# A hybrid two-layer trunk: one branch for steep decays of all heads, with its results in memory, instead of a branch in each head

## Chip, cores and metric

The kernel runs on one core of a Trainium2 chip. The metric is the device time of one execution in microseconds (us). Its engines are TensorE (PE, with its weight loads shown apart as PEld), VectorE (DVE), ScalarE (ACT), GpSimd (POOL) and SyncE (SP), which issues nearly all DMA transfers. The time before is 1061.45 us, the median of 3 runs (1060.91 to 1062.27).

## What is computed

Sixteen learned meta tokens are put ahead of 512 tokens of width 1024 (528 rows in all). Layer 1 is gated linear attention (GLA) with 4 heads, layer 2 differential softmax attention with 8 heads and a shared relative-position bias. Each has a pre-norm, an input projection, a SiLU gate and an output projection. All inputs are float32. What the change touches lies in the first layer:

```python
def gla_chunk(S, inp):
    q, k, v, lg = inp
    b = jnp.cumsum(lg, axis=2)                      # log decay, per key channel
    rel = b[:, :, :, None, :] - b[:, :, None, :, :]
    decay = jnp.exp(jnp.where(causal[:, :, None], rel, -jnp.inf))
    attn = jnp.einsum('bhid,bhjd,bhijd->bhij', q, k, decay)
    o = (jnp.einsum('bhij,bhjv->bhiv', attn, v)
         + jnp.einsum('bhid,bhdv->bhiv', q * jnp.exp(b), S))
    ...
```

and, in the second layer, in the bias `table[t5_bucket(max(dist, 0))]`, which the kernel makes as a matmul of the table with a constant 0/1 matrix (`c_hot`).

## The kernel before

Activations are kept transposed, channels on the 128 partitions and the 528 rows along the free axis. A product in float32 is made of three products of split operands (high x high, high x low, low x high): `split` (L238, L239) makes the high part on ACT and the low part on DVE, both for weights and for activations. The GLA projections of heads 1 to 3 are done as `Unit`s of seven half-size products (L355, 128 x 264 columns), so that sums of weight blocks are made on DVE as well (L295).

**Order.** PE's order is written out by hand. A `Weaver` object `W` holds a queue of generators that yield pieces of projection work. The code for the attention of a head calls `W.fill(us)`, which issues about that many us of projection matmuls, `W.finish(gen)`, which issues them up to the end of a generator, and `W.settle()`, which runs the work that was deferred (the turning of v into token order). The other engines get their order from a scheduler with priorities. Weights (`raw`) come in by SP one or two tiles ahead, when DVE has released the buffer.

**A head of GLA** (L1102 on): z of the head and q, k of the next are queued as filler; `gla_scores` makes the decayed keys kd (L986, L987) and the scores within blocks of 128 (L993, L1001), masked and split into `s.am` (16 meta rows) and `s.a`; `gla_ready` makes the scores across blocks from kd (L1018); `gla_blocks` makes the outputs. `gla_scores` uses exp(b) and exp(-b) as separate factors, which holds only while the decay within a block stays above a limit. So the kernel tests the least decay (`fl`, L871, L872), sums the flag over the partitions with a matmul (L875), puts it into `fi` (L877) and loads it into a register of each engine (L1101). In each of the four heads `tc.If(steep > 0)` (L1122, L1123 in the profile) stands between `gla_scores` and `gla_ready`; its body, `steep_scores`, makes the scores and kd again by eight levels of masks, and overwrites `s.am`, `s.a` and `s.kd`. It uses `hT`, the residual stream, as working space and saves it in `hT_dr`. With these inputs the flag is zero and the body never runs; each engine jumps past it.

**Second-layer setup** (`second_layer_setup`, in head 1): the 0/1 matrix comes in two halves of 33 x 328 (L893), then a matmul for each (L898), a copy and a store to `bdr`, and lam from four vectors (L902 on).

Of the kernel before, what the change touches and what calls it, by code (L numbers as in the profile page):

```python
# [11 lines left out]
F32 = mybir.dt.float32  # L12
# [7 lines left out]
P = 128  # L20
D = 1024
NM = 16
# [162 lines left out]
def trunk(ctx, tc, x, meta, g_norm, gla_w_in, gla_w_gate_up, gla_b_gate, gla_gnorm, gla_w_out,  # L185
# [35 lines left out]
    def ps_tile():  # L221
        return T(ps_pool, [P, 512], F32, "ps")
# [649 lines left out]
    dve.tensor_scalar(fl[:, 1:2], fl[:, 0:1], DECAY_LIMIT, None, op0=ALU.is_lt)  # L872
    W.fill(2.0)
    pf = ps_tile()
    pe.matmul(pf[0:1, 0:1], fl[:, 1:2], one1, start=True, stop=True)  # L875
    fi = T(hp, [1, 1], I32, "fi")
    dve.tensor_copy(fi, pf[0:1, 0:1])  # L877

    bdr = T(dp, [D_HEADS, TLEN], F32, "bdr")
    hT_dr = T(dp, [P, KT, L], F32, "hTd")
    lam = cp.tile([P, 1], F32, name="lam")
    dgs = cp.tile([P, 2], F32, name="dgs")

    def second_layer_setup():
        tab = T(cp, [NBUCK + 1, D_HEADS], F32, "tab")
        dve.memset(tab, NEG)
        sp.dma_start(tab[:NBUCK], rel_bias)
        n = TLEN // 2  # L890
        hots = [tmp(), tmp()]
        for i in range(2):
            sp.dma_start(hots[i][:NBUCK + 1, :n], c_hot[:, i * n:(i + 1) * n])  # L893
        W.fill(4.0)
        for i in range(2):
            hot, bsb = hots[i], tmp()
            ps = ps_tile()
            pe.matmul(ps[:D_HEADS, :n], tab, hot[:NBUCK + 1, :n], start=True, stop=True)  # L898
            dve.tensor_copy(bsb[:D_HEADS, :n], ps[:D_HEADS, :n])
            sp.dma_start(bdr[:, i * n:(i + 1) * n], bsb[:D_HEADS, :n])  # L900
        lamb, lt = tmp()[:, :4 * P].rearrange("p (a b) -> p a b", a=4), tmp()[:, :2 * P].rearrange("p (a b) -> p a b", a=2)
        sp.dma_start(lamb, d_lam.partition_broadcast(P))  # L902
        dve.tensor_tensor(lt, lamb[:, 0::2, :], lamb[:, 1::2, :], op=ALU.mult)
        lam2 = T(cp, [P, 2], F32, "lam2")
        dve.tensor_reduce(lam2, lt, axis=AX.X, op=ALU.add)
        act.activation(lam2, lam2, AF.Exp)
        dve.tensor_tensor(lam, lam2[:, 0:1], lam2[:, 1:2], op=ALU.subtract)
        dve.tensor_scalar(lam, lam, LAM_INIT, None, op0=ALU.add)
        dve.tensor_scalar(dgs, dg_sb, 0.5 * (1.0 - LAM_INIT), None, op0=ALU.mult)

    def steep_scores(hd, s):


        sp.dma_start(hT_dr, hT)
        flat = hT.rearrange("p k c -> p (k c)")
        qk = flat[:, :2 * L].rearrange("p (a b) -> p a b", a=2)
        raw = flat[:, 2 * L:2 * L + D].rearrange("p (k c) -> p k c", k=KT)
        acc = tmp()
        dve.memset(acc, 0.0)
        for i in range(2):  # L920
# [23 lines left out]
            act.activation(e[:, :400], e[:, :400], AF.Exp, scale=-1.0 / TAU)  # L944
            dve.tensor_tensor(s.kd[:, i, :], qk[:, 1, :400], e[:, :400], op=ALU.mult)
            for lv, half in enumerate(MASKS):
                mk = T(tp, [P, P], F32, "mk", bufs=1)
                sp.dma_start(mk, c_levels[lv])
                for t0, n, nb in ((0, NM, 1), (NM, NR, 4)):
# [24 lines left out]
                    dve.tensor_tensor(acc[:c, t0:t0 + n], acc[:c, t0:t0 + n], r[:c, :n], op=ALU.add)  # L974
        split(s.a[0], s.a[1], acc[:, NM:])
        pm = ps_tile()[:32, :NM]
        pe.matmul(pm, ident[:NM, :32], acc[:NM, :NM], start=True, stop=True)
        split3(s.am, pm, 64)
        sp.dma_start(hT, hT_dr)

    @urgent
    def gla_scores(hd, s):
        s.a = [T(gp, [P, NR], F32R, f"a{i}") for i in range(2)]
        s.kd = T(gp, [P, 2, 400], F32, "kd")
        for i in range(2):
            dve.tensor_scalar(s.kd[:, i, :NM], s.ks[:, i, :NM], eL[:, 2 * hd + i, 0:1], None, op0=ALU.mult)  # L986
            dve.tensor_tensor(s.kd[:, i, NM:].rearrange("p (b c) -> p b c", b=3),  # L987
                              s.ks[:, i, NM:400].rearrange("p (b c) -> p b c", b=3),
                              eL[:, 2 * hd + i, 1:4].unsqueeze(2).to_broadcast([P, 3, P]), op=ALU.mult)
        s.am = T(gp, [M3, NM], F32R, "am")  # L990
        pm = ps_tile()[:32, :NM]
# [3 lines left out]
        dve.tensor_tensor(r[:32, :NM], pm, short[:, :NM], op=ALU.mult)  # L995
        split3(s.am, r[:32, :NM], 64)
        ps = ps_tile()
        for b in range(4):
            cs = slice(NM + b * P, NM + (b + 1) * P)
            for i in range(2):  # L1000
                pe.matmul(ps[:, b * P:(b + 1) * P], s.ks[:, i, cs], s.qs[:, i, cs], start=i == 0, stop=i == 1)  # L1001
        r = tmp()[:, :NR]
        dve.tensor_tensor(r.rearrange("p (b c) -> p b c", b=4), ps.rearrange("p (b c) -> p b c", b=4),
                          tri.unsqueeze(1).to_broadcast([P, 4, P]), op=ALU.mult)
        split(s.a[0], s.a[1], r)

# [92 lines left out]
    token_sums(5)  # L1099
    W.settle()  # L1100
    steep = nc.values_load(fi[0:1, 0:1], min_val=0, max_val=P)  # L1101
    for hd in range(G_HEADS):  # L1102
        s = heads[hd]
# [12 lines left out]
        if hd == 0:  # L1116
            W.fill(3.0)
        gla_scores(hd, s)
        W.fill(4.0)
        if W.queue:  # L1120
            W.finish(W.queue[0])
        W.settle()  # L1122
        with tc.If(steep > 0):  # L1123
            steep_scores(hd, s)
        W.fill(2.0)
        gla_ready(hd, s)
        W.finish()
        W.settle()
# [410 lines left out]
```

## Time and profile before

| | us |
|---|---|
| median of 3 runs | 1061.45 |
| the profiled execution | 1060.68 |
| its span, first to last instruction | 1058.9 |
| PE busy | 1019.0 |
| DVE busy | 719.7 |
| ACT busy | 545.2 |

Mean granted clock of TensorE: 0.991 of full. A page of the profile gives busy times by engine; the timeline gives single instructions with the time that the engine stood idle before them and, behind an arrow, what ended that time. "PEq" and "DVEq" are the sequencers of PE and DVE, which read instructions, do branches and register loads, and hand the rest on. "L1123" rows are those of the branch: COMPARE_BRANCH is the jump, EVENT_SEMAPHORE what an engine does where both ways meet. In windows, PE busy is given with its count, the granted clock, the share of the DMA engines' time and GB/s.

### The profile page before, as it was taken

What the parts mean: (1) busy time and instruction counts of PE and PEld (TensorE: products, weight loads), DVE (VectorE), ACT (ScalarE), POOL (GpSimd) and SP (SyncE); (2) the same over time, 40 slices, a digit from 0 to 9 for tenths busy, and PEclk for the clock granted to TensorE, in tenths of its full rate; (3) what the DMA queues carried; (4) which work ended last, traced back from release to release, by engine and by line L of the source; (5) the groups of instructions that cost most, each with busy time, mean ns of one, the idle gap of its engine ahead of it and who ended that gap; (6) DMA issues with size and microseconds to landing.
All of it is one profiled execution on the core that took longest, in us unless ns stands there. A gap on an engine that the chain in (4) does not pass through costs nothing.

```text
span 1058.9 us, 18333 instructions
## 1 busy us (share of the span) xinstructions
PE 1019.0 (96%) x7345; PEld 954.2 (90%) x7345; DVE 719.7 (68%) x1441; ACT 545.2 (51%) x1198; POOL 38.4 (4%) x68
## 2 busy tenths in 40 slices
PE   8898988999899998999999999999999999999997
PEld 7898887999889997999999898998989989989895
DVE  7877884678776886656447675754757648576685
ACT  6774753446544655536525454443544445454453
POOL 1000000000000000000000000000000000000001
PEclk8999998999999999999999999999999999999999
DMA  7222221233212322212431222222222221222212
GB/s 195 64 56 69 80 82 55 79 81 81 82 41 80 92 68 82 81 48 77 130 105 45 89 81 90 80 90 81 80 88 61 89 93 54 88 80 81 72 48 80
DMA packets 98995, 84.69 MB, mean 80 GB/s; under 512 B 5528, under 2 KB 87802, under 8 KB 98892
## 3 DMA queue, kind: packets, MB, share of 16 engines
q1 hardware_dynamic: 98892, 83.31, 26.2%
q8 instruction: 65, 1.06, 0.4%
q14 instruction: 38, 0.31, 0.1%
HBM read 81.18 MB, written 2.12 MB: 79 GB/s over the span
## 4 chain that ended last, share of the span: by engine, by line
PE 57%; DVE 3%; ACT 1%; POOL 0%; issue 0%; POOLq 0%; DVEq 0%
PE pp L346 32%; PE pp L325 7%; PE ps L325 6%; PE bx L799 2%; PE bv L799 1%; PE bx L355 1%; PE by L799 1%; PE ps L1337 1%; PE ps L710 1%; PE bv L355 1%; PE ps L1360 1%; PE by L346 1%; PE ps L1018 1%; PE bv L346 1%; PE by L355 1%; DVE wl L239 0%
## 5 line engine op out<-in xcount | busy, mean ns | idle before, releaser
L346 PE MATMUL pp<-x,wh 128*128 128x264 f32 (+1 forms) x1504 | 321.7, 323 | 0.0
L346 PEld LDWEIGHTS pp<-x,wh 128*128 128x128 f32 x1504 | 227.0, 188 | 15.5
L238 ACT ACTIVATE wh<-raw 128x512 fp32r<-128x512 f32 (+1 forms) x212 | 138.2, 681 | 122.4 <-PE pp L346 52.6
L346 PE MATMUL pp<-x,wl 128*128 128x264 f32 (+1 forms) x752 | 198.2, 319 | 0.0
L239 DVE TENSOR_TENSOR wl<-raw,wh 128x512 fp32r<-128x512 f32 (+1 forms) x212 | 156.2, 757 | 56.6 <-ACT wh L238 41.2
L346 PEld LDWEIGHTS pp<-x,wl 128*128 128x128 f32 x752 | 124.3, 188 | 10.5
L457 POOL TENSOR_TENSOR st<-st,mhalf 128x1 f32<-128x1 f32 (+1 forms) x52 | 31.6, 607 | 942.8 <-DVE st L456 942.8
L1325 ACT ACTIVATE p<-p,st 128x528 f32<-128x528 f32 (+3 forms) x64 | 36.4, 569 | 49.3 <-DVE st L1324 48.9
L325 PE MATMUL pp<-wh,x 128*128 128x256 f32 x320 | 61.3, 282 | 0.0
L355 PE MATMUL bv<-x,wh 128*128 128x264 f32 x320 | 47.7, 287 | 4.9 <-DVE ks L400 2.5
L325 PEld LDWEIGHTS pp<-wh,x 128*128 128x128 f32 x320 | 51.0, 189 | 0.1
L355 PE MATMUL bx<-x,wh 128*128 128x264 f32 x320 | 48.3, 289 | 2.4 <-ACT u L374 1.2
L355 PEld LDWEIGHTS bv<-x,wh 128*128 128x128 f32 x320 | 42.3, 188 | 6.1 <-DVE ks L400 3.1
L355 PEld LDWEIGHTS bx<-x,wh 128*128 128x128 f32 x320 | 42.7, 190 | 3.2 <-issue 1.6
L325 PE MATMUL pp<-wl,x 128*128 128x256 f32 x160 | 45.1, 282 | 0.0
L1322 DVE SCALAR_TENSOR_TENSOR p<-ps,qr,T 128x264 f32<-128x264 f32 (+3 forms) x80 | 36.5, 490 | 6.4 <-PE ps L325 6.4
L374 ACT ACTIVATE u<-bx 128x264 f32<-128x264 f32 x60 | 23.0, 383 | 29.6 <-PE bx L355 28.6
L239 DVE TENSOR_TENSOR aT<-ps,aT 128x512 fp32r<-128x512 f32 (+3 forms) x32 | 15.7, 489 | 31.8 <-ACT aT L238 31.6
L325 PE MATMUL ps<-k,q 128*128 128x264 f32 (+3 forms) x240 | 36.8, 294 | 0.0
L325 PEld LDWEIGHTS ps<-k,q 128*128 128x128 f32 x240 | 33.6, 188 | 0.8
L325 PE MATMUL ps<-v,aT 128*128 128x256 f32 x240 | 33.9, 282 | 0.0
L325 PEld LDWEIGHTS ps<-v,aT 128*128 128x128 f32 x240 | 32.1, 188 | 1.8
(399 smaller groups left out, 2205.6 us busy)
## 6 DMA issues: line engine op xcount, KB each, us to landing
raw<-in_diff_w_in_dram SPq DMA_DIRECT2D x32, 1024.0 KB, 5.8
raw<-in_gla_w_in_dram SPq DMA_DIRECT2D x48, 512.0 KB, 5.3
raw<-in_gla_w_out_dram SPq DMA_DIRECT2D x8, 1024.0 KB, 5.1
raw<-in_diff_w_out_dram SPq DMA_DIRECT2D x8, 1024.0 KB, 5.0
T<-bdr SPq DMA_DIRECT2D x8, 264.0 KB, 3.6
out_dram<-z SPq DMA_DIRECT2D x8, 256.0 KB, 2.0
v<-in_x_dram SPq DMA_DIRECT2D x2, 512.0 KB, 6.7
qs<-in_x_dram SPq DMA_DIRECT2D x1, 512.0 KB, 3.8
```

The costliest lines, as they stand in the source:

```text
L238: act.activation(hi, src, AF.Copy)
L239: dve.tensor_tensor(lo, src, hi.bitcast(F32), op=ALU.subtract)
L325: pe.matmul(ps, l, r, start=first and n == 0, stop=last and n == 2, **kw)
L346: pe.matmul(bank, a[:, k, :], b[k][:, n0 + i * nn:n0 + (i + 1) * nn], start=k == 0 and n == 0, stop=k == nk - 1 and n == 2)
L355: pe.matmul(bank[:, :HT], w[p][:, k * P:(k + 1) * P], x[q][:, k, :], start=first and i == 0, stop=i == len(PASSES) - 1, skip_group_check=n ...
L374: act.activation(t, self.bx[:, :HT], AF.Copy, scale=self.sc)
L457: pool.tensor_tensor(dst, dst, mhalf[:np_, :dst.shape[1]], op=ALU.pow)
L710: pe.transpose(pt[:, b * P:(b + 1) * P], vt[:, t0:t0 + n], ident)
L799: pe.matmul(banks[i][:, :HT], h.t[p][:, k, mm * P:(mm + 1) * P], s.y[q][k][:, i * HT:(i + 1) * HT], start=n == 0, stop=n == len(PASSES) - 1)
L1018: pe.matmul(o, s.kd[:, i, kc], s.qs[:, i, t0:t0 + n], start=i == 0, stop=i == 1)
L1322: dve.scalar_tensor_tensor(p[:, c0:c1], ps[:, :c1 - c0], qr[:, b:b + 1], s.T[:, c0:c1], op0=ALU.mult, op1=ALU.add)
L1325: act.activation(p[:, :nk], p[:, :nk], AF.Exp, bias=st[:, m:m + 1], accum_out=st[:, 2 + m:3 + m])
```

## The change

1. The flag's matmul and its copy move from behind the decays to behind the projections of q and k of head 0, with `W.fill(1.0)` ahead and `W.fill(3.0)` behind, next to the register load.
2. One `tc.If(steep > 0)` stands there, ahead of the loop over heads. Its body saves `hT`, runs `steep_scores` for all four heads, and restores `hT`. `steep_scores` now writes scores and kd of a head to memory (`steep_dr`) in place of `s.a`, `s.am` and `s.kd`.
3. In `gla_scores` of each head, two DMAs are issued by SP with a condition on the flag's register: one into `s.kd` behind its making, one into the masked scores `r` ahead of their splits. The scores of the meta rows and of the blocks now lie in one tile `r`.
4. In the loop, `W.fill(4.0)`, the `W.finish` of the first generator, `W.settle()`, the branch and `W.fill(2.0)` become one `W.fill(5.0)`.
5. The 0/1 matrix is loaded whole, one head sooner, by one DMA into the buffer of kd, behind `gla_ready` of head 0.

```diff
@@ -870,16 +870,13 @@
-    W.fill(2.0)
-    pf = ps_tile()
-    pe.matmul(pf[0:1, 0:1], fl[:, 1:2], one1, start=True, stop=True)
     fi = T(hp, [1, 1], I32, "fi")
-    dve.tensor_copy(fi, pf[0:1, 0:1])
...
+    steep_dr = [[T(dp, shape, F32, f"steep{hd}_{i}") for i, shape in enumerate(([P, L], [P, 2, 400]))] for hd in range(G_HEADS)]
@@ -888,14 +885,11 @@
-        hots = [tmp(), tmp()]
-        for i in range(2):
-            sp.dma_start(hots[i][:NBUCK + 1, :n], c_hot[:, i * n:(i + 1) * n])
         W.fill(4.0)
         for i in range(2):
-            hot, bsb = hots[i], tmp()
+            bsb = tmp()
             ps = ps_tile()
-            pe.matmul(ps[:D_HEADS, :n], tab, hot[:NBUCK + 1, :n], start=True, stop=True)
+            pe.matmul(ps[:D_HEADS, :n], tab, hot[:NBUCK + 1, i * n:(i + 1) * n], start=True, stop=True)
@@ -972,11 +966,8 @@
-        split(s.a[0], s.a[1], acc[:, NM:])
-        pm = ps_tile()[:32, :NM]
-        pe.matmul(pm, ident[:NM, :32], acc[:NM, :NM], start=True, stop=True)
-        split3(s.am, pm, 64)
-        sp.dma_start(hT, hT_dr)
+        sp.dma_start(steep_dr[hd][0], acc)
+        sp.dma_start(steep_dr[hd][1], kd)
@@ -987,22 +978,23 @@
+        sp.dma_start(s.kd, steep_dr[hd][1], cond=steep > 0, cond_hint=False)
...
-        split3(s.am, r[:32, :NM], 64)
...
-        r = tmp()[:, :NR]
-        dve.tensor_tensor(r.rearrange("p (b c) -> p b c", b=4), ps.rearrange("p (b c) -> p b c", b=4),
+        dve.tensor_tensor(r[:, NM:].rearrange("p (b c) -> p b c", b=4), ps.rearrange("p (b c) -> p b c", b=4),
                           tri.unsqueeze(1).to_broadcast([P, 4, P]), op=ALU.mult)
-        split(s.a[0], s.a[1], r)
+        sp.dma_start(r, steep_dr[hd][0], cond=steep > 0, cond_hint=False)
+        split3(s.am, r[:32, :NM], 64)
+        split(s.a[0], s.a[1], r[:, NM:])
@@ -1098,7 +1090,18 @@
     W.finish(first[-1])
     token_sums(5)
     W.settle()
+    W.fill(1.0)
+    pf = ps_tile()
+    pe.matmul(pf[0:1, 0:1], fl[:, 1:2], one1, start=True, stop=True)
+    dve.tensor_copy(fi, pf[0:1, 0:1])
+    W.fill(3.0)
     steep = nc.values_load(fi[0:1, 0:1], min_val=0, max_val=P)
+    with tc.If(steep > 0):
+        sp.dma_start(hT_dr, hT)
+        for hd in range(G_HEADS):
+            steep_scores(hd)
+        sp.dma_start(hT, hT_dr)
@@ -1114,16 +1117,13 @@
         if hd == 0:
-            W.fill(3.0)
+            W.fill(2.0)
         gla_scores(hd, s)
-        W.fill(4.0)
-        if W.queue:
-            W.finish(W.queue[0])
-        W.settle()
-        with tc.If(steep > 0):
-            steep_scores(hd, s)
-        W.fill(2.0)
+        W.fill(5.0)
         gla_ready(hd, s)
+        if hd == 0:
+            hot = T(gp, [P, TLEN], F32, "kd")
+            sp.dma_start(hot[:NBUCK + 1], c_hot)
```

What this does to the order on the engines is shown at three places. The first is PE in head 0, at the jump. Before, the branch stood in the middle of a product of the next unit (bx, weights wh), behind the scores; the row behind COMPARE_AND_BRANCH here is the first one behind the body:

```order
L355 MATMUL bx_1203<-x_9_85,wh_1180 128x264 [waits Activation_49]
L355 MATMUL bx_1203<-x_10_86,wh_1180 128x264
L355 MATMUL bx_1203<-x_9_85,wh_1180 128x264
L1123 COMPARE_AND_BRANCH
...
L355 MATMUL bx_1203<-x_10_86,wh_1180 128x264
```

In the changed kernel the scores come behind the branch, and the register load stands right ahead of it:

```order
L355 MATMUL bv_1132<-x_7_83,wl_1057 128x264
L1098 TENSOR_LOAD fi_964 [waits DVE_49]
L1099 COMPARE_AND_BRANCH
...
L355 MATMUL bv_1132<-x_7_83,wl_1057 128x264 x3
L355 MATMUL bx_1073<-x_165_1077,wh_1065 128x264 [waits Activation_49]
...
L985 MATMUL ps_3957<-qs_821,ks_995 32x16 [waits DVE_49,PE_49]
```

The jump is 54 matmuls of 264 columns and the score matmuls earlier in PE's order than before, next to the load of the flag, and the first use of a PSUM tile behind it (ps) waits for DVE.

The second place is SP in head 1, where the table of the setup and the transfers of the head are issued. Before (t are the halves of the 0/1 matrix and the vectors of lam, raw a weight tile):

```order
L247 DMA raw_2575<-in_gla_w_out_dram 128x4x512 [waits DMAHW4_49,DMAHW7_49,DMAHW3_49,DVE_49]
L893 DMA t_2544<-in_hot_dram 33x328 [waits DMAHW0_49,PE_49]
L893 DMA t_2545<-in_hot_dram 33x328 [waits PE_49]
L902 DMA t_2617<-in_diff_lam_dram 128x512 [waits DMAHW0_49,PE_49]
L900 DMA bdr_1000<-t_2607 8x328 [waits DVE_49]
```

and in the changed kernel (the ISA rows make the condition; t_4707 is r):

```order
L247 DMA raw_4643<-in_gla_w_out_dram 128x4x512 [waits DMAHW1_49,DMAHW4_49,DMAHW0_49,DVE_49]
L981 ISA
L981 DMA kd_4697<-steep_1_146_970 128x800 [waits DMAHW7_49,DVE_49,PE_49]
L894 DMA bdr_965<-t_4675 8x328 [waits DVE_49]
L894 DMA bdr_965<-t_4680 8x328 [waits DVE_49]
L896 DMA t_4685<-in_diff_lam_dram 128x512
L995 ISA
L995 DMA t_4707<-steep_0_145_969 128x528 [waits DMAHW6_49,DVE_49]
L247 DMA raw_4787<-in_gla_w_out_dram 128x4x512 [waits DMAHW3_49,DMAHW2_49,DVE_49]
```

The loads of the table are gone from here, and two conditional transfers stand among the weight loads. The third place is ACT in head 1, behind the scores. Before, the splits into am and a waited for DVE alone:

```order
L332 ACTIVATE am_2634<-t_2638 32x16 [waits DVE_49]
L333 ACTIVATE am_2634<-t_2638 32x16
L238 ACTIVATE a_464_2627<-t_2652 128x512 [waits DVE_49]
```

In the changed kernel they wait for the DMA queue, and stand behind the split of the next weights (wh):

```order
L238 ACTIVATE wh_4779<-raw_4402 128x1024 [waits PE_49,Activation_49]
L332 ACTIVATE am_4703<-t_4707 32x16 [waits DMAHW1_49]
L333 ACTIVATE am_4703<-t_4707 32x16
L238 ACTIVATE a_906_4695<-t_4707 128x512
L238 ACTIVATE v_890_4646<-ps_4793 128x4x128 [waits PE_49]
L332 ACTIVATE cm_4805<-ps_4808 32x128 [waits PE_49]
```

What moved: am and a were made ahead of the branch and ahead of wh; now they come behind wh, behind a transfer, and ahead of v and cm.

More of the change, by code (lines that the diff above doesn't have):

```diff
@@ L909, in second_layer_setup, with steep_scores @@
         dve.tensor_scalar(dgs, dg_sb, 0.5 * (1.0 - LAM_INIT), None, op0=ALU.mult)
-    def steep_scores(hd, s):
-        sp.dma_start(hT_dr, hT)
+    def steep_scores(hd):
         flat = hT.rearrange("p k c -> p (k c)")
@@ L917, in steep_scores @@
         raw = flat[:, 2 * L:2 * L + D].rearrange("p (k c) -> p k c", k=KT)
-        acc = tmp()
+        kd = flat[:, 2 * L + D:2 * L + D + 800].rearrange("p (a b) -> p a b", a=2)
+        acc = flat[:, 3 * L + D + 400:4 * L + D + 400]
         dve.memset(acc, 0.0)
@@ L944, in steep_scores @@
             act.activation(e[:, :400], e[:, :400], AF.Exp, scale=-1.0 / TAU)
-            dve.tensor_tensor(s.kd[:, i, :], qk[:, 1, :400], e[:, :400], op=ALU.mult)
+            dve.tensor_tensor(kd[:, i, :], qk[:, 1, :400], e[:, :400], op=ALU.mult)
             for lv, half in enumerate(MASKS):
```

## The prediction

> **What bounds the kernel now.** I read the page first, then the chain of work, then the timeline of TensorE alone (PE) up to 500 us, and last the rows of the branch.
>
> ```profile
> span 1058.9 us, 18333 instructions
> PE 1019.0 (96%) x7345; PEld 954.2 (90%) x7345; DVE 719.7 (68%) x1441; ACT 545.2 (51%) x1198; POOL 38.4 (4%) x68
> ```
>
> PE is busy 1019.0 of 1058.9 us, and the chain that ended last runs almost wholly through PE matmuls, so time is won only where PE stands still or runs slowly. The timeline of PE prints, in brackets, how long it stood before a row and for whom. These are its stops in the stretch that the change touches:
>
> ```profile
> 80.75 0.19 PE L875 MATMUL ps<-ones,fl 128*1 128x1 f32 x2 [1.51 <-DVE fl L872]
> 86.89 1.40 PE L355 MATMUL bx<-x,a11h 128*128 128x264 f32 x8 [0.63 <-DVE ks L698]
> 102.74 0.85 PE L355 MATMUL bx<-x,wh 128*128 128x264 f32 x5 [1.18 <-PEq L1123]
> 107.33 1.25 PE L355 MATMUL bx<-x,wh 128*128 128x264 f32 x8 [1.23 <-ACT u L374]
> ...
> 159.49 1.26 PE L898 MATMUL ps<-t,tab 33*8 33x328 f32 x2 [2.87 <-DMA t<-in_hot_dram]
> 175.74 0.85 PE L355 MATMUL bv<-x,wh 128*128 128x264 f32 x5 [1.20 <-PEq L1123]
> 180.72 0.60 PE L1018 MATMUL ps<-qs,kd 128*32 128x128 f32 x4 [2.19 <-DVEq L1123]
> ...
> 287.95 0.84 PE L355 MATMUL bv<-x,wh 128*128 128x264 f32 x5 [1.22 <-PEq L1123]
> 292.36 0.60 PE L1018 MATMUL ps<-qs,kd 128*32 128x128 f32 x4 [1.62 <-DVEq L1123]
> ...
> 400.85 0.84 PE L355 MATMUL by<-x,a12h 128*128 128x264 f32 x5 [1.67 <-PEq L1123]
> 405.38 0.60 PE L1018 MATMUL ps<-qs,kd 128*32 128x128 f32 x4 [1.73 <-DVEq L1123]
> ```
>
> L1123 is the branch, taken past its body once for each of four heads. PE stops twice each time: while its own queue jumps (PEq), and then, in heads 1 to 3, until VectorE (DVE) has passed the branch too. Head 1 also waits 2.87 us for the table of L893. That stop has a second price, which the windows of PE show (length, PE busy, granted clock, DMA share, GB/s):
>
> ```profile
> 33.22:36.63 3.41, 1.45 (x9) 1.00 0.00 0
> 36.63:40.05 3.42, 3.42 (x18) 0.50 0.03 5
> ...
> 156.10:159.51 3.41, 0.54 (x6) 1.00 0.83 317
> 159.51:162.93 3.42, 3.42 (x12) 0.50 0.22 66
> 162.93:166.34 3.41, 3.41 (x18) 0.50 0.09 22
> ...
> 398.45:401.86 3.41, 1.74 (x15) 1.00 0.67 190
> 401.86:405.27 3.41, 1.79 (x15) 1.00 0.50 127
> ```
>
> After a window with 0.54 us of work, and after one with 1.45, the clock was 0.50 for one or two windows; after 1.74 it stayed at 1.00. In this trace the line lies between 1.45 and 1.74 busy out of 3.41.
>
> **What goes in heads 1 to 3.** The three branches go: 1.20 + 2.19 + 1.22 + 1.62 + 1.67 + 1.73 = **9.63 us** of PE idle time. The table is fetched some 40 us before its use, and L893's successor needs no transfer there: **2.87 us**. With that the emptied window is gone, and so are two windows at half clock, full of PE work: half of 6.83 is **3.4 us**. One group shows that this is real, the same 16 matmuls in head 0 and in head 1:
>
> ```profile
> 91.48 2.05 PE L1001 MATMUL ps<-qs,ks 128*128 128x128 f32 x16
> 162.09 3.78 PE L1001 MATMUL ps<-qs,ks 128*128 128x128 f32 x16
> ```
>
> This group alone gives 3.78 - 2.05 = 1.73 us, which is the low bound of the term. Sum of the three: 15.9 us. What is late next there is nothing large: the stops of 0.4 to 0.9 us at the changes between product units, which the branch does not cause, stay.
>
> **What happens in head 0.** The flag's matmul (L875) is put later, behind 12 more matmuls; fl is long done by then, and the stop of 1.51 goes. But the next stop, 0.63 for ks, comes from DVE, which was busy without a gap there, so PE only arrives sooner and waits longer: I take 1.3 in place of 0.63, so 0.65 is given back. Then comes the single branch, and it has to be priced anew, because it stands elsewhere.
>
> ```profile
> L1123 PEldq COMPARE_BRANCH  x4: 3292/3324/3756, 99.2 to 396.9; - x4
> L1101 PEldq TENSOR_LOAD <-fi x1: 491/491/491, 86.9 to 86.9; - x1
> ...
> L1123 ACTq COMPARE_BRANCH  x1: 50/50/50, 101.3 to 101.3; - x1
> L1123 ACTq EVENT_SEMAPHORE  x1: 17/17/17, 101.8 to 101.8; - x1
> L1123 DVEq COMPARE_BRANCH  x1: 67/67/67, 101.9 to 101.9; - x1
> L1123 DVEq EVENT_SEMAPHORE  x1: 21/21/21, 104.9 to 104.9; - x1
> ...
> L1123 DVEq COMPARE_BRANCH  x1: 63/63/63, 175.5 to 175.5; - x1
> L1123 DVEq EVENT_SEMAPHORE  x1: 21/21/21, 180.6 to 180.6; - x1
> ...
> q14 instruction: 38, 0.31, 0.1%
> ...
> 101.49:104.90 3.41, 2.23 (x19) 1.00 0.03 10
> ...
> 176.58:179.99 3.41, 1.95 (x17) 1.00 0.44 168
> ...
> 88.94 1.00 SPq L254 DMA_DIRECT2D raw<-in_gla_w_in_dram  x2
> ...
> 91.25:94.66 3.41, 3.41 (x32) 1.00 0.89 246
> ```
>
> PE's queue is some 2.2 us ahead of its engine (it reaches the branch at 99.2; its engine, full until then, restarts at 102.74 after 1.18 idle), so of 3.3 us 1.2 remain. Now the load of the flag stands right at the branch: with its 0.49 and about 0.1 between the two, PE idles 3.3 + 0.6 - 2.2 = 1.7 to 1.8. And the place is worse. DVE's jump took 3.0 us in head 0 (101.9 to 104.9) with DMA at 0.03, but 5.1 in head 1 (175.5 to 180.6) with a weight load under way at 0.44: instructions come over the DMA engines too (the queue of that kind), so what the jump has to fetch seems to queue with the data. The new branch comes, by my count of the rows ahead of it, at about 90 us, some 2 us after a pair of weight loads is issued (at 88.94 before, about 87.5 with the two kd operations now behind the split that releases the buffer); those loads fill the DMA for about 4 us. PE's own four jumps all began before the loads of their time. I add 0.9, near the middle between nothing and DVE's 2.1: **2.7 us** idle at the branch (bounds 1.2, as now, and 3.9).
>
> 2.7 us without work can leave a window under 1.45 us busy: 3.41 - 2.7 = 0.7 if the stop falls into one window, up to 2.0 if the border halves it. I take one window at half clock, **1.7 us** (bounds 0 and 3.4). The Trainium skill (TensorE: Matmul & The Clock Gate, section "What's actually happening") lets the clock fall only after at least one idle window of about 3.4 us. By that rule the new branch would cost no clock and the sum would be 1.7 us lower; the window from 33.22, with 1.45 us of work in it, speaks against the rule.
>
> Behind the branch PE's first use of a PSUM tile waits until DVE has passed; I take 0.5 for that. And ACT is late with u, as it was at 107.33 (1.23): the table load of L767 and the new wait stand ahead of it; I take 0.7. Head 0 in all: 1.51 + 1.18 + 1.23 = 3.9 saved; 0.65 + 2.7 + 1.7 + 0.5 + 0.7 = 6.25 paid.
>
> **The eight conditional transfers.** No run shows a transfer that is skipped. Nearest rows:
>
> ```profile
> t<-in_diff_lam_dram SPq DMA_DIRECT2D x1, 256.0 KB, 3.6
> raw<-in_diff_w_in_dram SPq DMA_DIRECT2D x32, 1024.0 KB, 5.8
> a<-in_gla_w_in_dram SPq DMA_DIRECT2D x1, 64.0 KB, 7.3
> ...
> 425.84 1.46 PE by L355 x12
> 94.30 0.64 ACT L238 ACTIVATE a<-t 128x512 fp32r<-128x512 f32 x1
> ```
>
> So a skip costs between nothing and 3.6 us from issue to release; I take 2, somewhat nearer to the transfer of a similar tile. The transfer of kd is issued right after kd is written, some 10 us ahead of its first reader on PE: hidden. That of the scores (r, a tile t) is issued about 1.2 us after the last score matmul, and three kinds of work stand behind it: ACT's am and a, then ACT's v, cm and u, then PE's product that reuses bx. In heads 1 to 3 PE has 69 matmuls of 264 columns before that product, 69 x 1.46 / 12 = 8.4 us, and two groups of transposes and the first kd products, about 2 us: 10.4. ACT needs, as I estimate, 3.3 us from the landing on (five 32-row copies, a at 0.64, v and u of like size). So a landing up to 7.1, a skip of 5.9 us, is free. I book 0.2 for each of the four heads, 0.8, for queueing; if the cover were gone, each skip would cost its 2 us. On SP's queue the weight loads behind these transfers wait for buffers that DVE releases later than it writes r, so nothing of theirs is delayed. The table's load, now one DMA of both halves into the kd buffer, stands behind head 0's last kd product; kd of head 1 then waits for PE to have read the table, which happens before DVE's turn.
>
> **Sum.** 15.9 + 3.9 - 6.25 - 0.8 = 12.8 us. The profiled execution took 1060.68 (span 1058.9 and 1.8 around it), so 1047.9; the median of the runs shown is 0.77 higher: **1048.7**. The stages behind 500 us are bound by PE and move as a whole.
>
> **Rivals.** (1) The clock holds at the new branch, since the border of the windows, free of the program, may halve the stop or the fetch may not queue: 1.7 less, **1047.0**. (2) The clock still falls in head 1: the matmuls of the table use 33 rows and 8 columns, and after the window from 159.51, full by its record, the clock stayed at 0.50; such work may not count. Then 3.4 comes back: **1052**. (3) The jump is far, now that one body holds four heads: ACT, which passed one head's body in 0.5 us (101.3 to 101.8), stops 3 to 5 us as DVE does now, is late with am, a, wh and u, and PE waits some 2 to 3 us more: **1051**. The Trainium skill (Runtime: NRT & Kernel Launch, section "Instruction fetch mechanics") says that a taken branch whose target lies outside the two pages held forces a fetch before anything goes on; ACT's 0.5 us fits a target that was held, and no run here shows ACT with a farther one. (4) Slower: the skip is no skip in time. Each r then blocks ACT's queue in its order, with PE's product behind it; free up to 5.9 us, beyond that 1 us for 1 us in four heads. It eats the 12.8 from 5.9 + 3.2 = 9.1 us on; at 10 us, **1065**. The longest landing above is 7.3, which speaks against it. (5) The branches' cost was not the branches': DVE is busy too (68% over the span), and PE arrives sooner at splits that are not ready; half of 9.6 returns: **1053.5**.
>
> **How the numbers follow.** Forecast 0.35, rival 1 0.26, rival 2 0.10, rival 3 0.13, rival 5 0.08, rival 4 0.05, and 0.03 that nothing moves. All good bounds together give 1061.45 - 15.9 - 3.9 + 1.2, about 1042.5; rivals 2, 3 and 5 and the high bounds reach to 1055. The range is 1043 to 1054.5. 0.2%, or 2.1 us, is about what a measurement of this kernel can tell from no change; faster than that 0.92, within it 0.03, slower 0.05.
>
> **What would show it.** PE's stops with L1123's successor as releaser: one group near 91 us, of 1.7 to 3.9 us, and none in heads 1 to 3. The windows of PE: clock 1.00 from 100 us on; 0.50 in the window behind the new branch or not decides between forecast and rival 1. ACT's idle time before am in heads 1 to 3 below 2 us, and the first kd product without a DMA as releaser. A stop of PE for u or bx of over 1 us in each head, or total PE idle time before 500 us down by less than 6 us, would make the prediction wrong.

## The result and the profile after

The changed kernel takes **1049.75 us** (median of 4 runs, 1044.26 to 1052.15); the kernel before took 1061.18 beside it (4 runs, 1059.28 to 1062.27). The ratio is 0.9892, with a 95% interval of 0.9870 to 0.9915: 11.4 us less. The prediction was 1048.7, in a range of 1043 to 1054.5. The profiled execution took 1049.57 us, 1060.68 before.

The page's first lines of the kernel after:

```profile
span 1047.8 us, 18311 instructions
PE 1017.8 (97%) x7345; PEld 954.0 (91%) x7345; DVE 718.8 (69%) x1441; ACT 544.5 (52%) x1198; POOL 37.9 (4%) x68
```

The same 7345 matmuls, 1.2 us less busy time, and a span that is 11.1 us shorter: what went is mostly time in which PE stood. The view by windows, cut at the same places in both kernels (the matmul that waits for DVE's ks in head 0, then the first stop at L799, the products of the output weights, behind the scores of heads 1, 2 and 3), shows where. Columns: window, its length, PE busy (instructions), granted clock, DMA share, GB/s. First before, then after:

```profile
0.00:86.89 86.89, 77.40 (x568) 0.94 0.40 104
86.89:189.53 102.64, 92.41 (x678) 0.97 0.23 67
189.53:301.15 111.62, 106.62 (x832) 1.00 0.27 77
301.15:438.14 136.99, 130.96 (x1025) 1.00 0.28 78
438.14:1058.90 620.76, 611.59 (x4245) 1.00 0.25 80
```

```profile
0.00:84.64 84.64, 75.30 (x566) 0.96 0.41 107
84.64:186.57 101.93, 95.60 (x695) 0.95 0.24 67
186.57:296.07 109.50, 106.79 (x831) 1.00 0.28 78
296.07:427.22 131.15, 128.60 (x1010) 1.00 0.29 81
427.22:1047.80 620.58, 611.49 (x4245) 1.00 0.25 80
```

From top to bottom: 2.25, 0.71, 2.12, 5.84 and 0.18 us less. The last row, over half of the span, did not move. The second and the fourth have to be read together: 16 kd matmuls, 2.4 us of work, came over from the fourth row into the second (x64 there before, x80 now, while the fourth went from x56 to x40). Without that shift heads 0 and 1 gained 3.1, head 2 gained 2.1 and head 3 gained 3.4. Heads 2 and 3 gained about what their branches had cost (2.84 and 3.40); heads 0 and 1 gained much less than the table and head 1's branch (9.7) would give. PE's timeline after shows why (its stops of over 1 us between 80 and 450 us):

```profile
84.64 1.24 PE L355 MATMUL bx<-x,a11h 128*128 128x264 f32 x8 [1.64 <-DVE ks L698]
94.35 1.00 PE L355 MATMUL bv<-x,wl 128*128 128x264 f32 x3 [3.65 <-PEq L1099]
167.12 1.34 PE L355 MATMUL bv<-x,wh 128*128 128x264 f32 x8 [1.80 <-DVE t L398]
```

No stop has the branch as releaser in heads 1 to 3, and none waits for the table. The three that remain are the earlier wait for ks, the single branch (L1099), and one that nobody had foreseen, in head 1 at 167.12. The windows of PE around the last two:

```profile
86.18:89.59 3.41, 3.41 (x30) 1.00 0.67 186
89.59:93.00 3.41, 1.11 (x10) 1.00 0.57 134
93.00:96.41 3.41, 2.06 (x9) 0.50 0.07 16
96.41:99.83 3.42, 3.42 (x19) 0.50 0.00 0
164.69:168.10 3.41, 1.61 (x14) 1.00 0.01 2
168.10:171.51 3.41, 3.41 (x18) 0.50 0.00 0
```

Both stops lowered the clock: two windows at 0.50 behind the branch, one in head 1. At half clock work takes about twice as long (the 16 score matmuls of the prediction: 3.78 us against 2.05), so a window costs about half of its PE time: 1.0 us for the first of the three, which holds 2.06 us of work, and 1.7 for each of the others.

The new stop's cause stands in DVE's and SP's timelines after:

```profile
160.06 0.55 DVE L978 TENSOR_TENSOR kd<-ks,eL 128x384 f32<-128x384 f32 x1
...
165.31 0.43 DVE L897 TENSOR_TENSOR t<-t 128x256 f32<-128x256 f32 x1 [3.89 <-DMA t<-in_diff_lam_dram]
...
166.66 0.41 DVE L398 SCALAR_TENSOR_TENSOR t<-bv,u 128x264 f32<-128x264 f32 x1
```

```profile
155.43 0.37 SPq L247 DMA_DIRECT2D raw<-in_gla_w_out_dram  x1
160.74 0.09 SPq L981 DMA_DIRECT2D kd<-steep  x1
161.04 0.69 SPq L894 DMA_DIRECT2D bdr<-t  x2
161.78 0.36 SPq L896 DMA_DIRECT2D t<-in_diff_lam_dram  x1
```

SP issues in order. The conditional transfer into kd (L981) may go only when DVE has written kd, at 160.06 + 0.55; behind it in the queue stand two stores of the table (L894), which wait for DVE's copies of it (until 161.42), and then the load of the four lambda vectors (L896), which needs nothing and goes out 5 us later than it could. This load was late in the kernel before, too: it went out at 160.78, and DVE stood 2.09 us for it, but PE, held up by the table, did not wait for that. Now DVE multiplies these vectors (L897) and stands 3.89 us for them first; behind that, in DVE's order, is L398, a step of a product whose result PE waits for.

### The profile page after: what moved, and what is told of

It reads as the page before. It is cut to its first block, busy times and chain, and to the rows that moved or that the text cites. A ratio compares the mean times of both kernels' runs of the same rounds, so it can differ in the third digit from the quotient of the medians.

```text
span 1047.8 us, 18311 instructions
## 1 busy us (share of the span) xinstructions
PE 1017.8 (97%) x7345; PEld 954.0 (91%) x7345; DVE 718.8 (69%) x1441; ACT 544.5 (52%) x1198; POOL 37.9 (4%) x68
## 3 DMA queue, kind: packets, MB, share of 16 engines
q1 hardware_dynamic: 98848, 83.31, 26.7%
HBM read 83.90 MB, written 2.12 MB: 82 GB/s over the span
## 4 chain that ended last, share of the span: by engine, by line
PE 77%; DVE 7%; ACT 2%; issue 2%; DMA 2%; POOL 1%; SPq 0%; POOLq 0%; DVEq 0%; ACTq 0%
PE pp L346 32%; PE ps L325 8%; PE pp L325 7%; PE bx L355 6%; PE bx L799 4%; PE bv L355 4%; PE by L355 3%; PE bv L799 2%; PE by L799 2%; PE ps L1010 2%; PE ps L710 1%; DMA raw<-in_gla_w_in_dram 1%; DVE wl L239 1%; PE ps L1337 1%; POOL st L457 1%
## 5 line engine op out<-in xcount | busy, mean ns | idle before, releaser
L239 DVE TENSOR_TENSOR wl<-sum,wh 128x1024 fp32r<-128x1024 f32 x20 | 24.4, 1221 | 14.5 <-ACT wh L238 9.6
```

The lines of the kernel that those rows point to most:

```text
L239: dve.tensor_tensor(lo, src, hi.bitcast(F32), op=ALU.subtract)
```

## The experiments

Each kernel was timed beside the kernel before. The last three columns are from the profiled execution alone: "branch" is PE's longest stop at the single branch in us, "windows" counts the half-clock windows between 80 and 450 us (1.7 us each where PE works through them), and "idle" is all the time in us that PE stands from the wait for ks in head 0 to the first L799 of head 3. The kernel before has two such windows and 21.3 us of idle time there, the kernel after three and 11.6.

| run | median us (range) | before beside it | ratio (95% interval) | branch | windows | idle |
|---|---|---|---|---|---|---|
| table only | 1055.28 (1053.69 to 1059.33) | 1059.46 | 0.9963 (0.9949 to 0.9977) | - | 1 | 18.6 |
| branch only | 1053.75 (1050.25 to 1055.13) | 1059.46 | 0.9940 (0.9920 to 0.9960) | 4.18 | 4 | 14.5 |
| no conditional transfers | 1047.07 (1045.53 to 1049.46) | 1059.46 | 0.9886 (0.9867 to 0.9905) | 3.95 | 1 | 10.7 |
| lambda sooner | 1047.11 (1043.94 to 1047.80) | 1059.46 | 0.9870 (0.9849 to 0.9890) | 4.21 | 1 | 12.1 |
| after again | 1048.86 (1046.79 to 1052.16) | 1059.95 | 0.9904 (0.9887 to 0.9922) | 3.48 | 1 | 11.3 |
| branch later | 1046.05 (1045.92 to 1046.86) | 1059.95 | 0.9868 (0.9852 to 0.9885) | 1.15 | 1 | 10.7 |
| empty body | 1040.53 (1039.52 to 1040.81) | 1059.95 | 0.9814 (0.9799 to 0.9828) | none | 0 | 6.2 |
| lambda sooner, branch later | 1042.98 (1042.24 to 1043.64) | 1059.95 | 0.9840 (0.9826 to 0.9855) | 1.15 | 0 | 8.9 |
| transfers run | 1051.47 (1049.62 to 1054.30) | 1059.53 | 0.9931 (0.9908 to 0.9954) | 3.74 | 2 | 13.7 |
| flag and branch later | 1047.65 (1044.88 to 1049.40) | 1059.53 | 0.9887 (0.9869 to 0.9905) | 2.25 | 0 | 12.5 |

**The table alone** (on the kernel before):

```
-        hots = [tmp(), tmp()]
-        for i in range(2):
-            sp.dma_start(hots[i][:NBUCK + 1, :n], c_hot[:, i * n:(i + 1) * n])
...
         gla_ready(hd, s)
+        if hd == 0:
+            hot = T(gp, [P, TLEN], F32, "kd")
+            sp.dma_start(hot[:NBUCK + 1], c_hot)
```

> The kernel before with one part of the change alone: the table of biases is fetched behind head 0's kd into the kd buffer; the four branches stay. Theory: the stop of 2.87 us for the table in head 1 goes, and with it the two windows at half clock behind it (3.4 us); nothing else moves: 6.3 us less than the kernel before, about 1054.9, and the 16 matmuls of L992's group in head 1 take about 2.05 us each row in place of 3.78. Rival A: the narrow matmuls of the table (33 rows, 8 columns) leave the clock to fall all the same: 2.9 us less, 1058.3. Rival B: the branch of head 1, 15 us later, takes back what PE gains, since DVE is late there: 1 us less or nothing.

Measured: 4.2 us less by the medians, between the theory and its first rival. The trace of this run decides (PE's timeline; the table's matmuls are L895, the group of 16 is L998):

```profile
155.43 1.27 PE L895 MATMUL ps<-kd,tab 33*8 33x328 f32 x4
156.85 2.05 PE L998 MATMUL ps<-qs,ks 128*128 128x128 f32 x16
...
395.54 0.85 PE L355 MATMUL by<-x,a12h 128*128 128x264 f32 x5 [1.56 <-PEq L1120]
400.08 0.60 PE L1015 MATMUL ps<-qs,kd 128*32 128x128 f32 x4 [1.74 <-DVEq L1120]
```

No stop and full speed in head 1: the 2.87 and the 3.4 us are gone, and the narrow table matmuls do not lower the clock. But in head 3 the two stops of the branch now fell into one window, and the clock was 0.50 for one window from 401.5. That is 1.7 us back, so by this count the edit gives 6.3 and this execution kept 4.6; its span is 4.2 less than that of the profile of the kernel before. The kernel before held its clock there by a hair (1.74 us of work in that window). So rival A falls, and rival B too: the two stops of the branch in head 1 were 1.68 and 1.36, no more than the 1.20 and 2.19 of before.

**The single branch alone**: the kernel after, with the two halves of the table loaded in the second layer's setup again (the lines with - of the diff above).

> The kernel after with the table's load put back to where it was (two halves, issued in the head that uses them): the single branch alone. Theory: the stop for the table (2.87 us) and its two windows at half clock (3.4 us) come back in head 1, but the stop of 1.80 us that the kernel after has a little later (score mask late, since DVE waited for the lambda vectors) is then covered by it: 2.8 to 6.3 us more than the kernel after, and 5 to 8.6 us less than the kernel before. Rival: the table is no part of the gain once the branches are gone: the time of the kernel after.

Measured: 5.7 us less than the kernel before, and by the ratios (0.9940 and 0.9904) 0.36%, or 3.8 us, more than the kernel after; the wait for the table (3.19 us at 162.68) and two half-clock windows from 162.0 are back, and L398 does not stop PE in head 1. Within the intervals the two parts of the change add up: 0.37% and 0.60% against 0.96% for both.

**No conditional transfers**: both lines `sp.dma_start(..., cond=steep > 0, ...)` in `gla_scores` are left out.

> The kernel after without the eight conditional transfers, so the results of the branch's body are left out. Theory: the transfer of kd stands on SP's queue ahead of the load of the lambda vectors and holds it until DVE has written kd; without it that load goes out sooner, DVE's wait of 3.9 us for it in head 1 goes, PE's stop of 1.80 us behind it and one window at half clock (1.7 us) go: about 3.5 us less than the kernel after. The skips themselves cost nothing that PE sees. Rival A (the 0.8 us booked for skips): 4.3 us less. Rival B: DVE is late there for another reason: the stop stays and the time is that of the kernel after.

**Lambda sooner**: all eight transfers stay.

```
 def second_layer_setup():
+        lamb = tmp()[:, :4 * P].rearrange("p (a b) -> p a b", a=4)
+        sp.dma_start(lamb, d_lam.partition_broadcast(P))
...
-        lamb, lt = tmp()[:, :4 * P].rearrange("p (a b) -> p a b", a=4), tmp()...
-        sp.dma_start(lamb, d_lam.partition_broadcast(P))
+        lt = tmp()...
```

> The kernel after with the load of the lambda vectors issued at the top of the second layer's setup, ahead of head 1's kd on SP's queue; all eight conditional transfers stay. Theory (one in-order queue, the skip holds what stands behind it): DVE's wait of 3.9 us goes, PE's stop of 1.80 us and the window at half clock behind it go: 3.5 us less than the kernel after, about 1046.2. Rival A: the vectors were only the last of several late things, and DVE's mask is late by 1 us all the same: 1 to 2 us less. Rival B: the skipped transfers themselves delay DVE or PE in each head: no change here, and a gain only where they are taken out.

Measured: 1047.07 and 1047.11, so no cost of the skipped transfers themselves shows beside the place of one load. SP's timeline without the transfers, and then with the load moved:

```profile
154.55 0.51 SPq L896 DMA_DIRECT2D t<-in_diff_lam_dram  x1
159.75 0.69 SPq L894 DMA_DIRECT2D bdr<-t  x2
```

```profile
155.95 0.51 SPq L889 DMA_DIRECT2D t<-in_diff_lam_dram  x1
160.84 0.09 SPq L982 DMA_DIRECT2D kd<-steep  x1
```

In both the load goes out some 5 us sooner, DVE does not stand for it (0.16 us in the second), and PE's stop in head 1 and its half-clock window are gone. Without the transfers the load also comes ahead of the table's stores in SP's order; "lambda sooner", which keeps the transfers, shows that its place alone does it. Against the kernel after (0.9904, in another set of runs) that is 0.2% to 0.3% less, with intervals that overlap, so the medians do not tell the theory's 3.5 us from rival A's 1 to 2; DVE's wait, gone in the trace, speaks for the theory's cause. The comparison within one set comes below. In this execution of "lambda sooner" a part went back: a stop of 1.76 us for L398 at 343.47, between the scores of heads 2 and 3, where the kernel after has 0.41. It is 1.69 in "flag and branch later" and under 0.6 in the other kernels with the single branch. DVE stands for a weight load just ahead of that step, 2.62 and 2.56 us in these two and 1.25 in the kernel after; why that load lands later was not tried.

**The branch's place.** The kernel after again, and four more units of other work ahead of the branch:

```
     steep = nc.values_load(fi[0:1, 0:1], min_val=0, max_val=P)
+    W.fill(4.0)
     with tc.If(steep > 0):
```

> The kernel after as it is, for a comparison on the chip of the three runs beside it. All theories: 11.4 us less than the kernel before, give or take 2; PE stops 3.65 us at the branch and 1.80 us in head 1.

> The kernel after with four more units of other work (about 4.4 us of PE) between the load of the flag and the branch, so that the weight transfers that were under way at the jump (DMA share 1.0 to 1.2 from 88 to 91 us) have landed. Theory (the jump's instruction fetch queues with the weights' data): PE's jump takes about 3.3 us in place of 5.2, as in the kernel before, PE idles 1.1 to 1.8 us in place of 3.65, and one window at half clock or none is left in place of two: 2 to 5 us less than the kernel after. Rival A (the jump is long because the body is four times as long, whatever the traffic): the jump stays near 5.2 us, PE idles 3 to 3.6, 0 to 0.6 us less. Rival B (idle PE is the price of the flag's load right at the branch): 0.5 us less, the jump at 5.2.

Here are the rows of the branch: of the kernel after, and of the one with the branch later.

```profile
L1099 PEldq COMPARE_BRANCH  x1: 5214/5214/5214, 89.0 to 89.0; - x1
L1099 ACTq COMPARE_BRANCH  x1: 50/50/50, 91.2 to 91.2; - x1
L1099 ACTq EVENT_SEMAPHORE  x1: 17/17/17, 94.8 to 94.8; - x1
```

```profile
L1100 PEldq COMPARE_BRANCH  x1: 3317/3317/3317, 94.7 to 94.7; - x1
L1100 ACTq COMPARE_BRANCH  x1: 50/50/50, 97.1 to 97.1; - x1
L1100 ACTq EVENT_SEMAPHORE  x1: 17/17/17, 99.7 to 99.7; - x1
```

The jump took 5.21 us while weight loads were under way (DMA share 1.06, 1.22 and 1.15 in the three microseconds from 88) and 3.32 with the DMA engines nearly idle; PE stood 3.65 and 1.15. Time: 2.8 us less than the kernel after on the same chip, within the theory's 2 to 5. Not all of that is PE's stop, though. Against "after again" the stop is 2.3 us shorter, but "idle" falls by 0.6 only: most of the gain comes back in smaller stops behind the branch and in head 2 (0.49 us at the scores, 0.40 and 0.30 for kd, 1.07 for ACT's t where it was 0.43). The rest is in the clock: the granted clock is 0.9915 in the mean of the six runs of "after again" and 0.9938 in the four runs here, some 2.4 us by my estimate (0.0023 of 1046). The one half-clock window of this profile lies ahead of the branch, behind the wait for ks, and shows how fine the line is:

```profile
81.95:85.37 3.42, 1.68 (x14) 1.00 0.00 0
85.37:88.78 3.41, 3.41 (x18) 0.50 0.33 78
```

Was it the traffic, or that the flag's load no longer stands right at the branch? The next kernel moves both (`W.fill(3.0)` ahead of `values_load` becomes `W.fill(7.0)`):

> The kernel after with the load of the flag and the branch both four units of work later: the flag is still loaded right at the branch, as in the kernel after, but the weight transfers have landed by then. It tells the traffic apart from the flag's load, which the run with the branch alone later had both moved. Theory (traffic): PE's jump 3.3 us in place of 5.2, PE idles 1.2 + 0.6 = 1.8 us in place of 3.65, no window or one at half clock. Rival (the flag's load right at the branch makes the jump long): the jump stays near 5.2 us and PE idles over 3 us.

```profile
L1099 PEldq COMPARE_BRANCH  x1: 3823/3823/3823, 94.6 to 94.6; - x1
...
98.55 0.61 PE L355 MATMUL by<-x,a22l 128*128 128x264 f32 x3 [2.25 <-PEq L1099]
```

The jump is 1.4 us shorter with the flag's load still in front of it, so the rival falls: it is not the flag's load that makes the jump long. The further 0.5 without it is no more than the spread of the jumps in the kernel before (3.29 to 3.76), and is not shown to be the load's. PE's stop follows the jump and the load together (3.65, 2.25, 1.15).

Both runs move PE's jump away from more than the weight loads, though. In the kernel after SP jumps at the same time (88.8 to 94.5), and other instructions are fetched. The profile shows instructions as DMA packets of queues of their own, 16 KB each on q8 and 8 KB on q14 (packets and MB of 90 to 92 us in the kernel after):

```profile
q8 instruction: 1, 0.02, 5.6%
q14 instruction: 2, 0.02, 2.8%
```

Each of PE's jumps in the kernel before has one packet of q8 in it. In "branch later" this packet starts 1.0 us into the jump and takes 0.96. In the kernel after it starts 2.0 us into the jump, at 90.99, as the weight data end and behind an earlier packet of its queue (from 89.89), and takes 1.80. In both the jump ends 1.4 us behind it, so the 1.9 us between them are this packet's. That weight data alone can hold such a packet is shown by DVE in the kernel before: its jump took 3.1 us in head 0 with no data on the DMA engines, and 5.0 in head 1, where weights filled them until 177.9, its packets started at 178.0, and the other engines' jumps were over. For PE's jump the shares of the weights, of the other engines' instructions and of the earlier packet on q8 are not told apart.

**The body emptied**: the loop over `steep_scores` and the conditional transfers are left out, two transfers of hT stay in the branch.

> The kernel after with the branch at its place but its body cut to the two transfers of hT, and without the eight conditional transfers: the steep results are left out. Weight transfers are under way at the jump as before. Theory (a jump has to fetch only what lies outside the instructions held; the fetch then queues with the weights): with the target near, the jump of every engine is short (0.5 us or less, as ACT's was in the kernel before), PE does not idle there and the clock stays at 1.00; with the stop of 1.80 us in head 1 gone too, as in the run without conditional transfers, 6 to 9 us less than the kernel after. Rival (a branch costs its 3 us and the traffic its 2, wherever the target lies): PE idles 3 to 4 us there, and only the 3.5 us of head 1 are gained.

```profile
L1097 PEldq COMPARE_BRANCH  x1: 231/231/231, 89.3 to 89.3; - x1
...
88.93:92.34 3.41, 3.41 (x31) 1.00 0.97 269
```

With the target near, PE's jump takes 0.23 us under the same traffic, and PE works through it without a gap. The time is 8.3 us less than that of the kernel after beside it, the largest gain of all runs. The two profiled executions are 6.7 us apart by their spans, and the trace of "after again" has this much in three places: the stop at the branch 3.48, the half-clock window behind it 1.7, the late lambda vectors 1.47. The rest of the 8.3 is in the other runs, whose clock was lower (0.9915 in the mean against 0.993 in the profiled one). So a branch as such costs PE nothing here; what costs is that the jump goes over a long body, and the traffic adds to what the jump then takes.

**Both, nothing left out**: "lambda sooner" and "branch later" together.

> The kernel after with the lambda vectors' load at the top of the second layer's setup and the branch four units of work later, nothing left out. Theory: the gains add: 3.5 us from head 1, 2 to 5 us from the branch; 1041 to 1044.5, if PE finds no new stop. Rival: DVE and ACT are late next, and PE's gained time returns at stops for t (a mask of the scores) and ks: 2 us less than the kernel after, no more than the earlier load alone.

Measured: 1042.98, with 1040.53 for the emptied body beside it (PE still stands 1.15 us at the branch). That is 3.1 us less than "branch later" on the same chip, and 5.9 less than the kernel after. Of the 3.1 the trace gives 1.67 to the late lambda vectors, PE's stop for L398 in "branch later". The half-clock window that "branch later" has and this run lacks lies ahead of the branch, so it is not theirs. Over the four traces in which they stop PE while the transfers are skipped, the vectors cost a stop of 1.47 to 1.80 us each time, and a half-clock window behind it (1.7) once, in the kernel after's own profile. The windows at the branch in this run:

```profile
92.59:96.01 3.42, 2.86 (x24) 1.00 0.03 9
96.01:99.42 3.41, 2.80 (x21) 1.00 0.05 14
```

No window falls. Of the rival (the gain returns at t and ks) a part shows: the stops for ks are what they were, and none for DVE's t in front of 450 us is over 0.7, but PE stands 1.38 us at 245.48 for ACT's t, where the kernel after has 0.57 and "after again" 0.43. It is the fastest of the kernels that leave nothing out, 1.6% (1.45% to 1.74%) faster than the kernel before.

**The transfers run each time**: the condition is dropped and the source is a piece of the output weights of the same size, so the scores and kd are other numbers.

> The kernel after with its eight conditional transfers run each time: same tiles, sizes and places, no condition, from rows of the output weights in memory, so the scores and kd are replaced by other numbers. Theory (the cover that the prediction worked out: a landing up to 5.9 to 7.1 us is free for the scores, some 10 us for kd): the transfers take about 4 us each (256 KB took 3.6, 512 KB 3.8), hidden; with the queueing on the DMA engines 0 to 2 us more than the kernel after. Rival (the chain from r by ACT to PE's next product has no such slack, and the weights behind are late): about 3 to 4 us in each of four heads, 12 to 16 us more than the kernel after.

```profile
kd<-in_gla_w_out_dram SPq DMA_DIRECT2D x4, 400.0 KB, 3.1
t<-in_gla_w_out_dram SPq DMA_DIRECT2D x4, 264.0 KB, 2.7
```

The transfers take about 3 us each, and in the other heads PE shows no stop for them: the one that is longer than in the kernel after, 1.33 us for ACT's t at 252.07, is 1.35 in "flag and branch later", where the transfers are skipped. In head 1 the stop for L398 is 2.68 (1.80 in the kernel after, 1.47 in "after again"), and the half-clock window behind it, with 2.87 us of work, is one that "after again" lacks. These 1.2 and 1.4 us are most of the 0.27%, or 2.9 us, by which it is slower than "after again"; the intervals overlap, so the theory's 0 to 2 us is not excluded. The rival's 12 to 16 us are out: the cover that the prediction worked out is there.

## Why the prediction was right, point by point

The direction, the size (12.8 us predicted, 11.1 in the profiled execution, 11.4 by the medians) and most of the places were right; several terms were off, and they partly cancel. That the total came so close is in part luck. By the windows above the forecast was 3.0 us too high for heads 0 and 1 and 0.7 for head 2, and 1.4 too low for the first stretch, where one half-clock window fewer fell by chance.

- **Heads 1 to 3, 9.63 us for the branches.** Gone; in the fourth window 3.4 against 3.40 predicted. In the third it is 2.1 against 2.84, since PE, arriving sooner, waits 0.57 for ACT's t where it hadn't before. Rival 5, that half would come back, did not come, though in some of the later kernels this wait for ACT's t is 1.07 to 1.38.
- **The table, 2.87 + 3.4 us.** Right, and shown by the table alone. Rival 2 fell. The 16 matmuls take 2.05 in head 1 too.
- **The wait for ks, 0.65 given back.** It was 1.0: 0.63 became 1.64.
- **The branch, 2.7 us idle.** The mechanism was right (a jump that fetches behind the weights' data), the size was too small: 3.65, and 3.48 to 4.21 over the six runs with the branch at this place. I had put the extra near the middle between nothing and DVE's 2.1; PE's jump took 1.9 more than in quiet (5.21 against 3.32), so the upper end was the better guess, and three of the six lie just beyond it. What else came in at that moment beside the weights is told under "flag and branch later".
- **The clock at the branch, one window.** One in four of the runs with the branch there, two in two (the kernel after's own profile and "branch only"). Rival 1, that the clock holds, came in none of them. The windows are free of the program: a border stood 1.35 us ahead of PE's restart behind the branch in the kernel after, and 1.34 behind it in "after again". How they cut the stop decides. The clock is also most of the scatter from 1044 to 1052: the granted clock was 0.996 in the run of 1044.26 us and 0.990 in that of 1052.15, which is some 6 of the 8 us; the profiles have two half-clock windows at the start of the span in some executions and three in others, and which fell in runs without a profile is not known. The Trainium skill (TensorE: Matmul & The Clock Gate, section "What's actually happening") lets the clock fall after an idle window; here it fell after windows with 1.61 and 1.68 us of work in 3.41, and held at 1.69 in "flag and branch later" (below). The sign that the prediction named, clock 1.00 from 100 us on, failed in head 1 at 168.10, behind the stop that the vectors cause.
- **Behind the branch, 0.5 for DVE and 0.7 for ACT's u.** Neither came. Rival 3's mechanism did: ACT's jump, 0.5 us before, took 3.6 (91.2 to 94.8). PE did not wait for it: its own jump ended only half a microsecond sooner (it restarts at 94.35), so nothing that ACT owed was late yet. The Trainium skill (Runtime: NRT & Kernel Launch, section "Instruction fetch mechanics") says that a taken branch to a target outside the pages held forces a fetch; the emptied body (0.23 us) against the full one (3.3 to 5.8) agrees with it.
- **The skips, 0.8 us for queueing: the step that failed.** A skip takes 0.09 us of SP, and the queue of the data moved as much as before (83.31 MB in both profiles), so the eight skips themselves are free, and the 2 us taken for one was too much. Where the transfers run each time, that queue moves 86.03 MB. But the prediction asked only which weight loads stand behind them and concluded that "nothing of theirs is delayed". The load that was delayed is that of the lambda vectors. It cost 1.80 us of idle PE and a half-clock window of 1.7 in this profile, and 1.5 to 1.7 without that window in the other traces.

For heads 0 and 1, behind the wait for ks, the terms came to 6.1 us: 9.66 for head 1's branch and the table and 2.41 for head 0's old stops, less 2.7, 1.7, 0.5, 0.7 and two skips of 0.2. Of that 3.5 were lost to the lambda vectors, 1.0 to the second window, which holds 2.06 us of work, and 0.95 to the longer jump; 1.6 came back from what was booked and did not happen (DVE, ACT's u, two skips). That leaves 2.2, and 3.1 were measured: some 0.5 of the rest is a stop for ks that was 0.77 before and is under 0.4 now, and about 0.4 I can't place. The first window's 2.25 us less holds one half-clock window that the kernel before had more in its execution, with 2.84 us of work, so 1.4, which is no effect of the change. One slip of the prediction changes nothing: its good bounds together give 1042.9, not 1042.5.

## What to carry to other kernels

A transfer that is skipped cost next to nothing here (0.09 us of SP), but its place in an in-order queue did: until its operands are ready it holds every load behind it, so loads that need nothing go ahead of it. A jump over the long body cost PE, DVE, ACT and SP 2.6 to 6.6 us each, so gather such branches into one, and put it where the DMA engines are quiet and each engine has a few microseconds of work queued. A stop can count twice when it leaves a clock window about half empty; look at the windows, not at the stops alone, and let several executions say how often the clock falls.

## What the runs showed of the hardware

- **The jump.** PE's jump over the body took 0.23 us with a near target (DMA share 0.97), 3.32 with a far one in quiet, 3.82 in quiet with the flag's load just ahead, and 5.05 to 5.78 with weight loads under way (six runs). For PE the body of four heads is no dearer than that of one: the kernel before took 3.29 to 3.76. For ACT it is: 0.6 to 0.9 us over one head's body, with no packet of instructions, and 2.6 over four in quiet (97.1 to 99.7 above).
- **The clock's line.** Below, the window of "flag and branch later" that held with 1.69 us of work in 3.41; 1.68 and 1.61 (above) fell. The borders of the windows are good to some 0.02 us, so between 80 and 450 us the line lies at about half of the window. It does not hold for every kind of work: in the first 25 us of each profile the clock fell behind windows with 2.0 to 2.5 us of recorded PE time (2.16 from 17.91 on in the kernel after), where matmuls stand singly between waits, and the cause is open. A window with 2.06 us of work at half clock did not bring the clock back, and one with 3.42 did (from 93.00 and 96.41, above); in the kernel before, one filled with the table's narrow matmuls (from 159.51) did not.

```profile
94.60:98.02 3.42, 1.69 (x14) 1.00 0.05 12
98.02:101.43 3.41, 2.88 (x24) 1.00 0.04 10
```

- **A skipped transfer** stands in the list of issues with its size, and moves nothing:

```profile
q1 hardware_dynamic: 98848, 83.31, 26.7%
...
kd<-steep SPq DMA_DIRECT2D x4, 400.0 KB
t<-steep SPq DMA_DIRECT2D x4, 264.0 KB
```
